# A fixed order for three engines in the second half of an output projection, with three modulation chunks moved behind it and one routing chain in place of two

## Chip, cores and metric

The kernel runs on one core of one Trainium2 chip. The metric is the device time of one execution in microseconds (us). The engines are TensorE (PE; PEld is its weight load), VectorE (DVE), ScalarE (ACT), GpSimd (POOL), and SyncE (SP), whose queue issues the loads of weights. Each engine executes its own list of instructions in order; what an instruction needs from another engine it awaits on a semaphore.

## What is computed

Two layers of a diffusion transformer on 256 latent tokens `x` and 256 context tokens `ctx`, width 1024. Each layer makes six modulation vectors for `x` and six for `ctx` out of the conditioning vectors, mixes tokens (layer 0: a gated linear recurrence beside a spatial gating unit, layer 1: latent attention), adds the result, and then runs a mixture of 32 experts in 4 groups of 8, two experts per token.

```python
for layer in range(DEPTH):
    mx = [m[:, None, :] for m in adaln(c, ada_w[layer], ada_b[layer])]     # 6 vectors
    mc = adaln(c_ctx, ada_w[layer], ada_b[layer])
    ...
    ox, oc = even_mixer(...)            # ends with "@ w_out"
    x = x + mx[2] * ox
    hx2 = modulate(rmsnorm(x, norm_ffn_g[layer]), mx[3], mx[4])
    ctx = ctx + mc[2] * oc
    hc2 = modulate(rmsnorm(ctx, norm_ffn_g[layer]), mc[3], mc[4])
    y = hier_moe(jnp.concatenate([hx2.reshape(-1, d), hc2.reshape(-1, d)], axis=0), *moe_args)
    ...
def hier_moe(...):                       # per token
    p_grp, grp = lax.top_k(softmax(hf @ w_r1 + b_r1), 1)          # 1 group of 4
    p_top, e_top = lax.top_k(softmax(logits2_of_that_group), 2)   # 2 experts of 8
    weight = p_grp * p_top / jnp.sum(p_top)
    ... gather rows by expert, (silu(g) * u) @ w_dn, weighted sum back
```

## The kernel before, in words

Tokens lie in four tiles of 128 (tiles 0 and 1 are `x`, tiles 2 and 3 are `ctx`). The program is written as if in one stream; a scheduler that simulates the engines then decides the order in which each engine's list is laid out, except inside a `manual_schedule` block, where the engines named keep the order in which the code is written.

**The modulations.** 24 chunks of the modulation weights (`ada_w`, 512 columns each, two loads of 1 MB) go through TensorE as many small products (`ada_chunk`, L399: 32 per chunk, then four at L407 for the bias). The accumulators are evacuated to `ada_r` (on ScalarE, or on VectorE with a gain), and GpSimd's queue writes the rows to a DRAM array `mod`. `todo` is the list of chunks, `adaq` those that are loading; `ada_next` runs one and starts the load of another.

**The output projection of layer 0** (L750 to L804) has two halves of 512 output columns. Each operand is split into a high and a low part, so that a product is three (`mm3`, L120 to L122). In the first half the loop runs over the contraction (8 chunks), with all four tiles inside it. In the second half the loop runs over tiles: per tile 8 times 3 products into `acc`, then

- `R.half(t)`: ScalarE squares the first half of the tile's row (L199), VectorE scales the sum (L200);
- `residual(t, 1, acc)`: VectorE multiplies the accumulators by the gate row (L776, `ymix`) and adds the product to the row (L777). A gate row comes by a DMA on ScalarE's queue (L773); there are four such rows for two buffers. In the first half the add is on GpSimd;
- `R.tile(t)`: square of the second half (L206), reciprocal root (L95 to L101), eight transposes (L213), two copies of them by ScalarE (L214, `h2T`), eight products with the router's weights (L217), and the logits (L218, `lg`);
- `R.rows(t, ...)`: the modulated row `h` (L229: VectorE; L230: the add of the shift `rS` on GpSimd), split into a copy by ScalarE and a difference by VectorE (L115 and L116; `hH` and `hL` of the order listings). `rA` and `rS`, the scale and shift rows, are DMAs on ScalarE's queue with one buffer each;
- after tile 3 `R.route`, once for tiles 0 to 2 and once for tile 3: some 30 small steps on VectorE that choose group and experts (`Mb` is the 0/1 table of choices), products that count each token's place in its expert's list (L277, L279, `prk`), the places `cm` (L281), and the weights `wsel`.

The last two chunks of modulations stand behind the loop (L803), and the scheduler may put them earlier.

**The experts** (`moe`). `one_hots(0)` makes the 0/1 matrix `P` from `cm` on VectorE (L856); `gather` (L881) picks rows by products with `P`; then pairs of experts in 16 steps: gate and up (L916), turn (L935), down (L1027), and every second step either a gather or a `combine` (L1046). Expert weights are loaded by SyncE (L849) into 13 buffers of 1 MB. In layer 0 four of these are free only when the projection's pool is closed; the other nine are shared with the chunks of modulations and with the projection's own weights.

Of the kernel before, what the change touches and what calls it, by code (L numbers as in the profile page):

```python
# [16 lines left out]
D = 1024  # L17
# [8 lines left out]
def body(ctx, tc, I, out, dbg=None, stop=None):  # L26
# [60 lines left out]
    def rsqrt(ss, n, inv, base=None):  # L87
# [9 lines left out]
        act(y, y, AF.Exp, scale=-0.5)  # L97
        V.tensor_tensor(a, y, y, op=OP.mult)
# [39 lines left out]
    class Router:  # L138
# [63 lines left out]
        def tile(self, t):  # L202

            cp, Q, c = self.cp, self.Q, t // 2
            ss = sm.tile([128, 1], F32, name="ss", bufs=4)
            act(junk_of(512), xs[t][:, 512:1024], AF.Square, accum_out=ss)  # L206
            rstd = rsqrt(ss, 1, 1.0 / D, self.v0[:, t:t + 1])
# [7 lines left out]
            pl = Q("bt")  # L215
            for k in range(KC):
                mm(pl[:, 0:40], xT[:, k, :], self.wA[c][:, k, :], start=k == 0, stop=k == KC - 1)  # L217
            V.scalar_tensor_tensor(self.lg[:, t, :], pl[:, 0:40], rstd, self.bS[c], op0=OP.mult, op1=OP.add)  # L218
            return rstd

        def rows(self, t, rstd, hs, A=None, S=None):
# [13 lines left out]
        def route(self, t0, t1):  # L235
# [38 lines left out]
            prk = Q("bt", (128, 4, 32))  # L274
            for i in range(NT):
                t = t0 + i
                mm(prk[:, i, :], before, Mb[:, t, :], start=i == 0, stop=t == 0, skip_group_check=True)  # L277
                for u in range(t):
                    mm(prk[:, i, :], ones, Mb[:, u, :], start=False, stop=u == t - 1, skip_group_check=True)  # L279
            cm = self.cm[:, ts]  # L280
            V.scalar_tensor_tensor(cm, prk[:, 0:NT, :], 1.0, Mb[:, ts], op0=OP.add, op1=OP.mult)  # L281

            ge = small([4], "gex")
            V.tensor_tensor(ge, lg[:, :, 0:4], m1[:, :, 0:1].to_broadcast([128, NT, 4]), op=OP.subtract)
            act(ge, ge, AF.Exp)
            gs, gmax = small([1], "gs"), small([1], "gmax")
            V.tensor_reduce(gs[:, :, 0], ge, axis=AX.X, op=OP.add)
            V.tensor_reduce(gmax[:, :, 0], ge, axis=AX.X, op=OP.max)
            V.reciprocal(gs, gs)
            V.tensor_tensor(gs, gs, gmax, op=OP.mult)  # L290
            w1, w2, hw = small([5], "w1"), small([5], "w2"), small([5, 8], "l3")
            V.tensor_tensor(w2, m2, m1, op=OP.subtract)
            act(w2, w2, AF.Exp)
            V.tensor_scalar(w1, w2, 1.0, None, op0=OP.add)
            V.reciprocal(w1, w1)
            V.tensor_tensor(w1, w1, gs.to_broadcast([128, NT, 5]), op=OP.mult)
            V.tensor_tensor(w2, w1, w2, op=OP.mult)
            for h, w in ((hb, w1), (h2, w2)):
                src = h1 if h is hb else h2
                V.tensor_tensor(h.rearrange("p t g e -> p (t g) e"), src.rearrange("p t g e -> p (t g) e"),  # L300
                                w.rearrange("p t g -> p (t g)")[:, :, None].to_broadcast([128, NT * 5, 8]), op=OP.mult)
            V.tensor_tensor(fl(hw), fl(hb), fl(h2), op=OP.add)
            chosen(self.wsel[:, ts], hw)
# [28 lines left out]
    def even_layer(HL, main):  # L332
# [6 lines left out]
        with ExitStack() as st:  # L339
# [53 lines left out]
            def ada_chunk(l, c, w, cols=None):  # L393

                g, half = divmod(c, 2)
                pa = P("ad")
                for k in range(KC):
                    for j in range(4):
                        mm(pa[32 * j:32 * j + 32, 0:128], cst[:, k, :], w[k // 4][:, k % 4, j * 128:(j + 1) * 128],  # L399
                           start=k == 0, stop=cols is not None and k == KC - 1, skip_group_check=True)  # L400
                r = ap.tile([128, 128], F32, name="ada_r", bufs=2)
                if cols is not None:
                    act(r, pa[:, 0:128], AF.Copy)
                    tp(cols[:, c, :], r, ident)
                    return
                for j in range(4):
                    mm(pa[32 * j:32 * j + 2, 0:128], sbi[:, l * 12 + c, :], adab[:, j * 128:(j + 1) * 128],  # L407
                       start=False, stop=True, skip_group_check=True)
                if (l, g) in gains:
# [68 lines left out]
            todo = [(0, c) for c in range(4, 12)] + [(1, c) for c in range(12)]  # L478
# [7 lines left out]
            def ada_next():  # L486
                ada_chunk(*adaq.pop(0))
                ada_ahead()
# [274 lines left out]
        with ExitStack() as st:  # L763
# [714 lines left out]
```

## Time and profile before

| what | value |
|---|---|
| time, median of 3 runs | 1541.81 us (1540.93 to 1544.79) |
| the profiled execution | 1538.64 us, its span 1536.9 us |
| granted TensorE clock, mean | 0.977 of full speed |
| PE busy | 1435.8 us (93% of the span) |
| DVE busy | 662.7 us (43%) |
| ACT busy | 432.5 us (28%) |
| POOL busy | 224.9 us (15%) |
| first product of the second half of layer 0's output projection | 338.7 us |
| first product of the first gather of layer 0's experts | 392.77 us |
| first product with expert weights in layer 0 | 402.36 us |

The span runs from the first to the last instruction; 1.7 us lie around it. The table's last three lines are starts on TensorE, from the span's start. A busy TensorE is not one at its peak: matmuls overlap, and the same matmul takes about twice as long when the granted clock is 0.50.

### The profile page before, as it was taken

To read this page: it belongs to the slowest core of one execution; us is meant where nothing else is said; L and a number is where in the kernel's file an instruction comes from. 1 tells how busy PE (TensorE), PEld (TensorE's weight loads), DVE (VectorE), ACT (ScalarE), POOL (GpSimd) and SP (SyncE) were. 2 spreads that over 40 slices of the span, in tenths; PEclk is the share of its full clock that TensorE was granted. 3 is DMA by queue.
4 is the path that set the end of the run, shared out by engine and by line. 5 is a ranking of instruction groups with operands and counts; after the bars stand their busy time and mean duration, and the time that the engine had idled before them with its cause. 6 is when DMAs were issued, how large, how long until landed. Compare 5 with 4: busy or idle time off the path is not lost. (4 is left out here: it accounts for less than half of the span.)

```text
span 1536.9 us, 21613 instructions
## 1 busy us (share of the span) xinstructions
PE 1435.8 (93%) x8526; PEld 836.2 (54%) x8526; DVE 662.7 (43%) x1494; ACT 432.5 (28%) x984; POOL 224.9 (15%) x250
## 2 busy tenths in 40 slices
PE   6989999999799999999999988997999989999987
PEld 5767777868444554554535356886344434334443
DVE  4455546767424334244423455666232323222222
ACT  4433334543111111211112144453122212212212
POOL 2222222123002012022203221101010100010010
PEclk9999999999899999999999999998999999999999
DMA  9775344785899999999899853135999999999995
GB/s 354 230 248 162 114 144 159 289 298 202 352 406 420 419 421 419 419 420 420 362 417 381 334 226 104 53 99 204 404 420 420 420 419 421 420 421 420 420 420 207
DMA packets 126051, 495.22 MB, mean 322 GB/s; under 512 B 17739, under 2 KB 38636, under 8 KB 77816
## 3 DMA queue, kind: packets, MB, share of 16 engines
q1 hardware_dynamic: 119704, 487.33, 80.3%
q10 hardware_dynamic: 2192, 3.72, 0.7%
q0 software_dynamic: 4048, 2.73, 0.6%
q8 instruction: 70, 1.15, 0.3%
q14 instruction: 37, 0.30, 0.1%
HBM read 492.59 MB, written 1.13 MB: 321 GB/s over the span
## 5 line engine op out<-in xcount | busy, mean ns | idle before, releaser
L916 PE MATMUL gu<-w,xT 128*64 128x512 f32 x2048 | 456.6, 597 | 19.1 <-DMA w<-in_moe_w_gu_dram 13.2
L916 PEld LDWEIGHTS gu<-w,xT 128*64 128x64 f32 x2048 | 151.6, 138 | 313.5 <-issue 273.6
L1027 PE MATMUL dn<-w,hh 128*64 128x512 f32 x960 | 220.2, 606 | 0.0
L924 DVE COPY hh<-gu 128x256 f32<-128x256 f32 x64 | 27.2, 425 | 363.2 <-ACT junk L923 363.2
L1050 POOL TENSOR_TENSOR xx<-xx,z 128x512 f32<-128x512 f32 x56 | 72.8, 1323 | 754.8 <-DVE z L1049 754.8
L1027 PEld LDWEIGHTS dn<-w,hh 128*64 128x64 f32 x960 | 73.7, 139 | 125.1 <-issue 117.9
L923 ACT ACTIVATE junk<-gu 128x256 f32<-128x256 f32 x64 | 24.5, 384 | 397.4 <-PE gu L916 397.4
L120 PE MATMUL mm<-WH,hH 128*128 128x512 f32 x288 | 116.5, 407 | 0.7 <-ACT hH L115 0.7
L121 PE MATMUL mm<-WL,hH 128*128 128x512 f32 x288 | 115.0, 400 | 1.4 <-DVE WL L116 1.4
L122 PE MATMUL mm<-WH,hL 128*128 128x512 f32 x288 | 112.0, 398 | 0.0
L1017 DVE SCALAR_TENSOR_TENSOR y<-dn,ws,y 128x512 fp32r<-128x512 f32 x60 | 45.0, 751 | 145.9 <-ACT y L1016 143.8
L1046 PE MATMUL ad<-y,PT 128*128 128x512 f32 x368 | 95.1, 405 | 5.3 <-DVE z L1049 4.2
L1016 ACT ACTIVATE y<-dn,ws 128x512 fp32r<-128x512 f32 x60 | 41.2, 687 | 176.2 <-PE dn L1027 166.1
L1046 PEld LDWEIGHTS ad<-y,PT 128*128 128x128 f32 x368 | 66.1, 188 | 35.9 <-issue 13.0
L116 DVE TENSOR_TENSOR WL<-w,WH 128x512 fp32r<-128x512 f32 x76 | 56.6, 752 | 54.9 <-ACT WH L115 51.5
L115 ACT ACTIVATE WH<-w 128x512 fp32r<-128x512 f32 x80 | 48.4, 627 | 109.9 <-PE mm L122 86.6
L1049 DVE TENSOR_TENSOR z<-ad,gt 128x512 f32<-128x512 f32 x100 | 66.1, 683 | 14.3 <-PE ad L1046 9.1
L399 PE MATMUL ad<-w,cst 128*32 128x128 f32 x1536 | 60.6, 284 | 6.7 <-DMA w<-in_ada_w_dram 6.7
L120 PEld LDWEIGHTS mm<-WH,hH 128*128 128x128 f32 x288 | 54.8, 190 | 16.9 <-issue 4.0
L121 PEld LDWEIGHTS mm<-WL,hH 128*128 128x128 f32 x288 | 54.8, 190 | 13.0 <-DVE WL L116 1.5
L122 PEld LDWEIGHTS mm<-WH,hL 128*128 128x128 f32 x288 | 54.1, 189 | 12.9 <-issue 1.6
L414 POOL DMA_DIRECT2D mod<-ada_r x80 | 40.4, 512 | 140.1 <-ACT ada_r L412 126.0
(434 smaller groups left out, 1962.3 us busy)
## 6 DMA issues: line engine op xcount, KB each, us to landing
w<-in_moe_w_gu_dram SPq DMA_DIRECT2D x256, 1024.0 KB, 16.3
w<-in_moe_w_dn_dram SPq DMA_DIRECT2D x120, 1024.0 KB, 12.2
w<-in_ada_w_dram SPq DMA_DIRECT2D x48, 1024.0 KB, 7.4
w<-in_ev_w_in_dram SPq DMA_DIRECT2D x32, 256.0 KB, 4.3
w<-in_moe_w_dn_dram SPq DMA_DIRECT2D x16, 512.0 KB, 12.0
w<-in_ev_w_in_dram SPq DMA_DIRECT2D x6, 1024.0 KB, 5.0
w<-in_ev_w_out_dram SPq DMA_DIRECT2D x4, 1024.0 KB, 6.9
w<-in_od_w_out_dram SPq DMA_DIRECT2D x4, 1024.0 KB, 5.1
```

The lines of the kernel that those rows point to most:

```text
L115: act(H, src, AF.Copy)
L116: (eng or V).tensor_tensor(L, src, H, op=OP.subtract)
L120: mm(out, lh, rh, start=start, stop=False, skip_group_check=True)
L121: mm(out, lh, rl, start=False, stop=False, skip_group_check=True)
L122: return mm(out, ll, rh, start=False, stop=stop, skip_group_check=True)
L399: mm(pa[32 * j:32 * j + 32, 0:128], cst[:, k, :], w[k // 4][:, k % 4, j * 128:(j + 1) * 128], start=k == 0, stop=cols is not None and k == ...
L916: mm(gu[64 * c:64 * c + 64, :], xT[:, k, base:base + CAP], w[:, c], start=k == 0, stop=k == KC - 1)
L1017: V.scalar_tensor_tensor(y[:, 1], py, ws, y[:, 0], op0=OP.mult, op1=OP.subtract)
L1027: mm(py[c][64 * par:64 * par + 64, :], hT[par][:, k // 2, k % 2, :], w_[par][:, k % 2, c * 512:(c + 1) * 512], start=k == 0, stop=k == 3)
L1046: mm(cb, PT[:, t, :], y[c][:, i % 2], start=i == 0, stop=i == 2 * len(pend) - 1)
L1049: V.tensor_tensor(z, cb, gate[t // 2][:, hs_], op=OP.mult)
L1050: (V if n % 4 == 3 else nc.gpsimd).tensor_tensor(xs[t][:, hs_], xs[t][:, hs_], z, op=OP.add)
```

## The change

The loop over tiles of the second half becomes one block in which PE, DVE and ACT keep the written order:

- TensorE runs the tiles one after another, `project(t)`, with the transposes (`turn`) and router products (`logits_mm`) of earlier tiles at written places between them.
- The add of the shift `rS` moves from GpSimd to VectorE; `rows` becomes a generator, so that its four steps can be placed one by one. Tile 3's are spread over the tail.
- `rA` and `rS` are issued on GpSimd's queue (`mod_rows`), no longer on ScalarE's.
- One chunk of modulations (`ada_next`) runs before the block, and the last three are kept: the sums of the first in two halves around tile 3's router products, the other two behind it, all ahead of the counting products (`place`). To have three, a third chunk is loaded into buffers of the pool `wxa`, which expert weights used so far. The order of chunks is changed too, so that the last three need no gain and are evacuated by ScalarE.
- `route` is cut into `choose` (with `rest`, the weights) and `place`, and runs once for all four tiles.
- The first `one_hots(0)` of the experts gets high priority. Layer 1's router is written with the new functions; its instructions stand as before.

```diff
@@ even_layer, the second half of the output projection
-            rows, w, WH, WL = {}, ahead[0], [], []
-            for t in range(4):
-                c = t // 2
-                if t % 2 == 0:
-                    rows[c] = (bcast_row(cp, mod[0, 4, c], D, "rA"), bcast_row(cp, mod[0, 3, c], D, "rS"))
-                acc = P("mm")
-                for k in range(KC):
...
-                    mm3(acc, tok(cH, k, t), tok(cL, k, t), WH[k], WL[k], k == 0, k == KC - 1)
-                R.half(t)
-                residual(t, 1, acc)
-                rstd = R.tile(t)
-                if t == 3:
-                    R.route(0, 3)
-                    R.route(3, 4)
-                R.rows(t, rstd, HL.tile(...), *rows[c])
+            mod_rows(0)
+            rstd, rows, xT = {}, {}, {}
+            ada_next()
+            if todo:
+                ada_ahead(wxa[0])
+            assert len(adaq) == 3 and not todo, (len(adaq), len(todo))
+            with tc.manual_schedule(engines={mybir.EngineType.PE, mybir.EngineType.DVE, mybir.EngineType.Activation}):
+                project(0, 0, KC)
+                for t in range(2):
+                    R.half(t)
+                project(1, 0, KC)
+                pl = {}
+                for t in range(4):
+                    residual(t, 1, acc[t])
+                    if t > 1:
+                        R.logits_out(t - 2, rstd[t - 2], pl[t - 2])
+                    ss = R.square(t)
+                    rstd[t] = rsqrt(ss, 1, 1.0 / D, R.v0[:, t:t + 1])
+                    if t == 3:
+                        pl[2] = R.logits_mm(2, xT[2])
+                        xT[3] = R.turn(3)
+                        break
+                    for _ in rows_of(t):
+                        pass
+                    xT[t] = R.turn(t)
+                    if t < 2:
+                        R.half(t + 2)
+                        project(t + 2, 0, KC)
+                        pl[t] = R.logits_mm(t, xT[t])
+                    if t == 1:
+                        mod_rows(1)
+                rows = rows_of(3)
+                next(rows)
+                next(rows)
+                l, c, wc = adaq.pop(0)
+                pa = P("ad")
+                ada_sums(l, c, wc, pa, 0, 4)
+                pl[3] = R.logits_mm(3, xT[3])
+                ada_sums(l, c, wc, pa, 4, KC)
+                for t in (2, 3):
+                    R.logits_out(t, rstd[t], pl[t])
+                next(rows)
+                sums = l, c, pa
+                rest = R.choose(0, 4)
+                while sums:
+                    ada_out(*sums)
+                    sums = ada_chunk(*adaq.pop(0)) if adaq else None
+                next(rows, None)
+                R.place(0, 4)
+            rest()
@@ Router.rows
-            nc.gpsimd.tensor_tensor(h2, h2, S, op=OP.add)
+            yield
+            V.tensor_tensor(h2, h2, S, op=OP.add)
...
-            split(h2, hs[:, 0, :], hs[:, 1, :])
+            yield
+            act(hs[:, 0, :], h2, AF.Copy)
+            yield
+            V.tensor_tensor(hs[:, 1, :], h2, hs[:, 0, :], op=OP.subtract)
```

**Where the rows stand now.** The first place is on ScalarE: the DMA of the fourth gate row, which the residual of tiles 2 and 3 needs (`junk,ss` are squares, `w` is the buffer of the context tiles, `h2T` the copies of transposes). Before:

```order
L773 DMA gate<-mod 128x512
L199 ACTIVATE junk,ss<-xx 128x512
L773 DMA gate<-mod 128x512
L206 ACTIVATE junk,ss<-xx 128x512
L199 ACTIVATE junk,ss<-xx 128x512
L206 ACTIVATE junk,ss<-xx 128x512
L96 ACTIVATE rs_y<-rs_v 128x1
L199 ACTIVATE junk,ss<-w 128x512
L97 ACTIVATE rs_y<-rs_y 128x1
L96 ACTIVATE rs_y<-rs_v 128x1
L97 ACTIVATE rs_y<-rs_y 128x1
L214 ACTIVATE h2T<-bt 128x512 x2
```

And of the change:

```order
L96 ACTIVATE rs_y<-rs_v 128x1
L97 ACTIVATE rs_y<-rs_y 128x1
L256 ACTIVATE hL_3683<-h_3684 128x1024
L226 ACTIVATE h2T<-bt 128x512 x2
L201 ACTIVATE junk,ss<-w 128x512
L818 DMA gate<-mod 128x512
L214 ACTIVATE junk,ss<-w 128x512
L96 ACTIVATE rs_y<-rs_v 128x1
L97 ACTIVATE rs_y<-rs_y 128x1
L256 ACTIVATE hH_3763<-h_3764 128x1024
```

The fourth gate's DMA stood before all second-half squares and ahead of the copies; now it stands behind tile 1's `hL` copy and transposes.

The second place is on VectorE: from tile 0's residual on. Before:

```order
L776 TENSOR_TENSOR ymix<-mm,gate 128x512 x2
L777 TENSOR_TENSOR xx<-xx,ymix 128x512
L776 TENSOR_TENSOR ymix<-mm,gate 128x512
L777 TENSOR_TENSOR xx<-xx,ymix 128x512
L95 SCALAR_TENSOR_TENSOR rs_v<-ss,v_767 128x1
L200 TENSOR_SCALAR v_767<-ss 128x1
L95 SCALAR_TENSOR_TENSOR rs_v<-ss,v_767 128x1
L200 TENSOR_SCALAR v_767<-ss 128x1
L98 TENSOR_TENSOR rs_a<-rs_y 128x1
L99 TENSOR_TENSOR rs_a<-rs_a,rs_v 128x1
L98 TENSOR_TENSOR rs_a<-rs_y 128x1
L100 TENSOR_SCALAR rs_a<-rs_a 128x1
```

And of the change:

```order
L821 TENSOR_TENSOR ymix<-mm,gate 128x512
L822 TENSOR_TENSOR xx<-xx,ymix 128x512
L95 SCALAR_TENSOR_TENSOR rs_v<-ss,v_767 128x1
L100 TENSOR_TENSOR rs_a<-rs_y 128x1
L101 TENSOR_TENSOR rs_a<-rs_a,rs_v 128x1
L102 TENSOR_SCALAR rs_a<-rs_a 128x1
L103 TENSOR_TENSOR rs_y<-rs_y,rs_a 128x1
L250 SCALAR_TENSOR_TENSOR h_3611<-xx,rs_y,rA 128x1024
L252 TENSOR_TENSOR h_3611<-h_3611,rS 128x1024
L258 TENSOR_TENSOR hH_3610<-h_3611,hH_3610 128x1024
L202 TENSOR_SCALAR v_767<-ss 128x1
L821 TENSOR_TENSOR ymix<-mm,gate 128x512
```

The reciprocal roots of tiles 0 and 1 were woven into each other; now tile 0 is carried to the end, shift add and split included, before tile 1's residual begins.

The third place is on TensorE: from the last product of the projection to the counting products. Before:

```order
L213 MATMUL bt<-ident,w 128x128 x8
L399 MATMUL ad<-w,cst 32x128 x17
L407 MATMUL ad<-adab,sbi 2x128 x4
L217 MATMUL bt<-wA_3416,h2T 128x40 x4
L213 MATMUL bt<-ident,w 128x128 x2
L217 MATMUL bt<-wA_3416,h2T 128x40 x4
L213 MATMUL bt<-ident,w 128x128 x6
L399 MATMUL ad<-w,cst 32x128 x16
L217 MATMUL bt<-wA_3416,h2T 128x40 x8
L399 MATMUL ad<-w,cst 32x128 x16
L407 MATMUL ad<-adab,sbi 2x128 x4
```

And of the change:

```order
L235 MATMUL bt<-wA_3407,h2T 128x40 x8
L225 MATMUL bt<-ident,w 128x128 x8
L235 MATMUL bt<-wA_3416,h2T 128x40 x8
L225 MATMUL bt<-ident,w 128x128 x8
L441 MATMUL ad<-w,cst 32x128 x16
L235 MATMUL bt<-wA_3416,h2T 128x40 x8
L441 MATMUL ad<-w,cst 32x128 x16
L447 MATMUL ad<-adab,sbi 2x128 x4
L441 MATMUL ad<-w,cst 32x128 x32
L447 MATMUL ad<-adab,sbi 2x128 x4
L441 MATMUL ad<-w,cst 32x128 x32
L447 MATMUL ad<-adab,sbi 2x128 x4
```

Behind tile 3's router products stood 16 products of a chunk and its bias; now there stand 16, 32 and 32 products of three chunks, each with its bias.

## Rows read from the trace of the kernel before

**Rows 1.** Stretches: us, busy us by engine, granted PE clock, DMA share, GB/s.

```profile
342.00:369.30 27.30, 27.30 (x132) 22.34 (x132) 19.96 (x37) 7.98 (x22) 9.35 (x8) 0.94 0.59 232
...
379.40:386.80 7.40, 7.40 (x87) 6.03 (x77) 6.42 (x33) 1.58 (x4) 2.40 (x2) 0.50 0.59 220
...
392.77:396.30 3.53, 3.53 (x16) 3.53 (x17) 1.28 (x2) 0.00 (x0) 0.20 (x1) 0.50 0.92 358
396.50:402.36 5.86, 5.86 (x53) 5.79 (x52) 1.38 (x2) 0.60 (x1) 0.14 (x1) 1.00 1.00 420
402.36:756.00 353.64, 349.50 (x1798) 170.40 (x1795) 126.97 (x214) 68.81 (x157) 40.93 (x30) 1.00 1.00 415
```

**Rows 2.** TensorE's waits, 402 to 756 us: total us, times, longest.

```profile
PE bt L935 <- DVE hh L927: 2.1, 1, 2.1
...
PEld gu L916 <- DMA w<-in_moe_w_dn_dram: 1.1, 4, 0.3
```

**Rows 3.** TensorE in order of time: start, us (a product of f32 operands counts twice).

```profile
365.22 1.87 PE L217 MATMUL bt<-wA,h2T 128*128 128x40 f32 x16
...
373.01 1.28 PE L399 MATMUL ad<-w,cst 128*32 128x128 f32 x34
...
380.77 3.64 PE L217 MATMUL bt<-wA,h2T 128*128 128x40 f32 x16
384.34 1.94 PE L399 MATMUL ad<-w,cst 128*32 128x128 f32 x32
386.21 0.60 PE L407 MATMUL ad<-adab,sbi 24*2 24x128 f32 x8
...
390.94 0.21 PE L277 MATMUL bt<-Mb,before 128*128 128x32 bf16 x1 [3.38 <-DVE Mb L269]
...
392.77 0.80 PE L881 MATMUL ad<-P,hH 128*128 128x256 f32 x2 [1.54 <-DVE P L856]
...
402.36 13.95 PE L916 MATMUL gu<-w,xT 128*64 128x512 f32 x64
```

**Rows 4.** VectorE in order of time: start, us, instruction, idle before.

```profile
347.43 0.68 DVE L776 TENSOR_TENSOR ymix<-mm,gate 128x512 f32<-128x512 f32 x1
352.66 0.69 DVE L776 TENSOR_TENSOR ymix<-mm,gate 128x512 f32<-128x512 f32 x1 [4.55 <-issue]
...
360.33 3.46 DVE L229 SCALAR_TENSOR_TENSOR h<-xx,rs_y,rA 128x1024 f32<-128x1024 f32 x1
...
372.28 0.68 DVE L777 TENSOR_TENSOR w<-w,ymix 128x512 f32<-128x512 f32 x1
...
373.75 1.45 DVE L95 SCALAR_TENSOR_TENSOR rs_v<-ss,v 128x1 f32<-128x1 f32 x1 [0.62 <-ACT junk L206]
...
376.82 1.28 DVE L229 SCALAR_TENSOR_TENSOR h<-w,rs_y,rA 128x1024 f32<-128x1024 f32 x1
378.02 1.22 DVE L116 TENSOR_TENSOR hH<-h,hH 128x1024 fp32r<-128x1024 f32 x1
...
379.44 0.28 DVE L259 TENSOR_REDUCE m<-lg 128x15 f32<-128x120 f32 x1
...
384.45 0.26 DVE L218 SCALAR_TENSOR_TENSOR lg<-bt,rs_y,bS 128x40 f32<-128x40 f32 x1 [0.83 <-PE bt L217]
...
391.50 1.22 DVE L856 TENSOR_TENSOR P<-iota,cm 128x1024 fp32r<-128x1024 f32 x1
```

**Rows 5.** ScalarE in order of time: start, us, instruction.

```profile
373.00 0.63 ACT L206 ACTIVATE junk<-w 128x512 bf16<-128x512 f32 x1 [2.71 <-DVE w L777]
...
375.91 1.04 ACT L115 ACTIVATE hH<-h 128x1024 fp32r<-128x1024 f32 x1
...
377.38 1.08 ACT L214 ACTIVATE h2T<-bt 128x512 f32<-128x512 f32 x2 [0.25 <-PE bt L213]
```

**Rows 6.** GpSimd in order of time: the shift add of one tile.

```profile
360.31 2.40 POOL L230 TENSOR_TENSOR h<-h,rS 128x1024 f32<-128x1024 f32 x1 [10.24 <-DVE rs_y L101]
```

**Rows 7.** The tile `gate`: from a DMA's issue to its landing.

```profile
DMA to landing us min/median/max: 3.7/5.2/6.7
```

More of the change, by code (lines that the diff above doesn't have):

```diff
@@ L97, in rsqrt @@
         act(y, y, AF.Exp, scale=-0.5)
+        if mid is not None:
+            mid()
         V.tensor_tensor(a, y, y, op=OP.mult)
@@ L229, in rows, with place, choose @@
             V.scalar_tensor_tensor(h2, xs[t], rstd, A, op0=OP.mult, op1=OP.mult)
-            nc.gpsimd.tensor_tensor(h2, h2, S, op=OP.add)
+            yield
+            V.tensor_tensor(h2, h2, S, op=OP.add)
             if t == 0:
                 dump(f"h2_{self.l}", h2)
-            split(h2, hs[:, 0, :], hs[:, 1, :])
-        def route(self, t0, t1):
+            yield
+            act(hs[:, 0, :], h2, AF.Copy)
+            yield
+            V.tensor_tensor(hs[:, 1, :], h2, hs[:, 0, :], op=OP.subtract)
+        def place(self, t0, t1):
+            Mb = self.Mb
+            prk = self.Q("bt", (128, 4, 32))
+            for t in range(t0, t1):
+                i = t - t0
+                mm(prk[:, i, :], before, Mb[:, t, :], start=i == 0, stop=t == 0, skip_group_check=True)
+                for u in range(t):
+                    mm(prk[:, i, :], ones, Mb[:, u, :], start=False, stop=u == t - 1, skip_group_check=True)
+            V.scalar_tensor_tensor(self.cm[:, t0:t1], prk[:, 0:t1 - t0, :], 1.0, Mb[:, t0:t1], op0=OP.add, op1=OP.mult)
+        def choose(self, t0, t1):
             NT, cp, Q, lg, l = t1 - t0, self.cp, self.Q, self.lg[:, t0:t1], self.l
@@ L272, in route @@
             chosen(Mb[:, ts], hb)
[L274 to L301, printed above, removed]
@@ L305, in blocks @@
+            return rest
         def blocks(self, cp, Q):
@@ L399, in ada_chunk, with ada_sums @@
                         mm(pa[32 * j:32 * j + 32, 0:128], cst[:, k, :], w[k // 4][:, k % 4, j * 128:(j + 1) * 128],
-                           start=k == 0, stop=cols is not None and k == KC - 1, skip_group_check=True)
+                           start=k == 0, stop=k == KC - 1, skip_group_check=True)
                 r = ap.tile([128, 128], F32, name="ada_r", bufs=2)
-                if cols is not None:
-                    act(r, pa[:, 0:128], AF.Copy)
-                    tp(cols[:, c, :], r, ident)
+                act(r, pa[:, 0:128], AF.Copy)
+                tp(cols[:, c, :], r, ident)
+            def ada_sums(l, c, w, pa, k0=0, k1=KC):
+                for k in range(k0, k1):
+                    for j in range(4):
+                        mm(pa[32 * j:32 * j + 32, 0:128], cst[:, k, :], w[k // 4][:, k % 4, j * 128:(j + 1) * 128],
+                           start=k == 0, stop=False, skip_group_check=True)
+                if k1 < KC:
                     return
+                g, half = divmod(c, 2)
                 for j in range(4):
@@ L408, in ada_chunk, with ada_out @@
                        start=False, stop=True, skip_group_check=True)
+                return l, c, pa
+            def ada_out(l, c, pa):
+                g, half = divmod(c, 2)
+                r = ap.tile([128, 128], F32, name="ada_r", bufs=2)
                 if (l, g) in gains:
@@ L476, in load_head @@
                 return r
-            todo = [(0, c) for c in range(4, 12)] + [(1, c) for c in range(12)]
+            todo = [(0, c) for c in range(4, 12)] + [(1, c) for c in (8, 9, 0, 1, 2, 3, 4, 5, 6, 7, 10, 11)]
             adaq = []
@@ L783, in even_layer, with mod_rows, project @@
                 residual(t, 0, acc0[t])
[L784 to L790 removed]
+            w, WH, WL, acc = ahead[0], [], [], {}
+            rA, rS = {}, {}
+            def mod_rows(c):
+                rA[c], rS[c] = (bcast_row(cp, mod[0, i, c], D, n, eng=nc.gpsimd) for i, n in ((4, "rA"), (3, "rS")))
+            def project(t, k0, k1):
+                if k0 == 0:
+                    acc[t] = P("mm")
+                for k in range(k0, k1):
                     if t == 0:
@@ new lines, in rows_of @@
+            def rows_of(t):
+                return R.rows(t, rstd[t], HL.tile([128, 2, D], F32R, name=("hH0", "hL0", "hH1", "hL1")[t]), rA[t // 2], rS[t // 2])
+            mod_rows(0)
[47 more added lines that the diff above has]
+                R.place(0, 4)
@@ L1419, in odd_layer @@
                     rstds.append(R.tile(t))
-                R.route(0, 2)
+                rest = R.choose(0, 2)
+                R.place(0, 2)
+                rest()
                 for t in range(2):
-                    R.rows(t, rstds[t], HL.tile([128, 2, D], F32R, name=f"s{t}"))
+                    for _ in R.rows(t, rstds[t], HL.tile([128, 2, D], F32R, name=f"s{t}")):
+                        pass
         return R
```

55 lines of the change are left out of this document (45 added, 10 removed).

## Prediction

> **What bounds the kernel now.** I read the stretches first, to see which engine is full where. From 402.36 us on, the first twelve steps of layer 0's experts keep TensorE busy for 349.5 of 353.6 us [rows 1], and TensorE's waits say that nearly none of the rest is for weights: the longest wait is 2.1 us for VectorE, those for loads sum to 1.1 us [rows 2]. DMA is full there too (share 1.00, 415 GB/s), but it is ahead. So whatever moves the first expert product at 402.36 moves everything behind it by as much; a stretch ahead of it is worth its full length.
>
> Next, how that product comes about. TensorE is full through the second half of the projection, 27.3 of 27.3 us [rows 1], that is 6.8 us per tile. After it the line of work leaves TensorE: tile 3's row is complete at 372.96 (the add at 372.28) [rows 4], its router products run 380.77 to 384.41 at the lower clock [rows 3], its logits stand at 384.45, `P` at 391.50 [rows 4], the gather begins at 392.77 and lasts 9.6 us [rows 3]. The granted clock in these stretches is what the reader should note: 0.50 (1.2 GHz) from 379.4 to 396.3, and 1.00 (2.4 GHz) after [rows 1].
>
> **The change, part by part.** I carry the line of work from tile 0 to the gather, with durations of the rows.
>
> *Tile 0 starts sooner.* TensorE no longer runs tiles 0 and 1 in turns. VectorE was idle for 4.55 us before tile 0's residual at 352.66, and its last work ahead of it ends at 348.1 [rows 4]. TensorE's list now gives it tile 0's 24 products alone, so the residual can start at 348.1. I allow 0.6 us for GpSimd's adds of the first half: a VectorE operation with two operands in SBUF took 3.46 us instead of 1.28 beside GpSimd's add at 360.31 [rows 4, 6]. Tile 0's row is complete at 348.1 + 0.6 + 2 x 0.7 = 350.1 instead of 354.1: a gain of 4.0 us.
>
> *Each tile is now one closed chain on VectorE.* From a complete row to the next one, in written order: square on ScalarE and the way to `rs_v` 0.8 (372.96 to 373.75); `rs_v` itself 0.15 (1.45 less the 1.3 for which GpSimd held it); root and its four corrections 1.62 (375.20 to 376.82); `h` 1.28; the shift add, now on VectorE, 1.22 by the row of its size; ScalarE's copy 1.04; the difference 1.22; the next tile's multiply and add 1.4 [rows 4, 5]. Sum 8.7 us. In the schedule before, pieces of other tiles filled these gaps; now VectorE idles through them. The shift add itself is a gain: GpSimd took 2.40 for it and could hold VectorE by up to 2.2 [rows 4, 6].
>
> Two of the three passages cost more. VectorE scales the first-half square of the tile after next before it goes on, and ScalarE makes that square behind the two copies of transposes: 1.08 + 0.8 against the 1.22 of VectorE's difference, 0.7 late [rows 4, 5]. Tile 1 is complete at 350.1 + 9.4 = 359.5, tile 2's chain is due at 368.9.
>
> *The fourth gate row comes late.* Its DMA is now behind tile 1's copies on ScalarE (order, first place), so it is issued just when VectorE wants the row. Landing takes 3.7 to 6.7 us [rows 7]; queued behind VectorE's wait are tile 2's residual and all that follows. I take 4.4, toward the low end, because the projection's weights are all in by then and the queue is quiet. Tile 2 is complete at 373.3, tile 3 with its 8.7 and one logits step of 0.26 at 382.3, against 372.96 before: 9.3 us later.
>
> *Router products and the kept chunks.* Behind tile 3's row: square, root, two copies of transposes, 0.8 + 0.15 + at most 1.3 of the 1.62 + 1.08 = 3.4 us, then the router products. TensorE by then has had some 10 us with little to do, since its last projection product comes by 348.1 + 3 x 6.8 = 368.5; in the trace its clock fell at 379.4 though it had been busy for most of the ten microseconds before. So 3.64 us, as in the row, and not 1.87 [rows 3]. Tile 3's logits stand at 382.3 + 3.4 + 3.6 + 0.3 = 389.6.
>
> Then TensorE has, ahead of the counting products, 16 + 32 + 32 products with three biases (order, third place). A trace row counts each twice, so a chunk is two rows of 32. At the lower clock 5 x 1.94 + 3 x 0.60 = 11.5, and 0.6 for two handovers of the one accumulator: 401.4. At the upper clock 160 x 0.038 + 3 x 0.4 + 0.6 = 7.9: 397.2 [rows 3].
>
> VectorE meanwhile has the chain of choices for four tiles: twelve steps in series of 0.28 to 0.35, ten small ones between at half of that, four masks: about 5.5; then tile 3's difference 1.22 and the weights 1.2, which stand ahead of `cm`: 397.5 [rows 4]. One chain in place of two saves VectorE some 3 us of steps, but nothing now waits for it longer than for TensorE.
>
> From the counting products to the gather it is 392.77 - 390.94 = 1.8 us before [rows 3]; with twice the products 2.3. Lower clock: 401.4 + 2.3 = 403.7, which is **10.9 us** later. Upper clock: VectorE decides, 397.5 + 0.3 + 1.3 = 399.1, **6.3 us** later.
>
> I take the lower clock. The row that is nearest is 379.40 to 386.80: TensorE was busy for all 7.40 us with just these chunk and router products, and the clock stayed 0.50; it rose only during the gather [rows 1]. The Trainium skill, "TensorE: Matmul & The Clock Gate", Part 1, says the opposite for dense work: the throttled state is the default and activity releases it. By that rule three chunks in a row bring the clock up and 6.3 is the result; the trace does not bear it out for this mixture, but no row has two whole chunks without router products between them.
>
> *At nothing:* `rA` and `rS` on GpSimd's queue (wanted 8 us after issue; if late, the landing of a gate row's size again, 4 us); layer 1's router (rows unchanged); the high priority (`P` stood first before). The third chunk takes two load buffers early, and six are kept until its sums: 6 MB, 15 us at 415 GB/s [rows 1]. The last two come free at about 401 and are wanted by the second expert 7 us after the first product at 413, so they are hidden; uncovered they would cost 5.
>
> **Sum.** The profiled execution took 1538.64 us. With 10.9 it would be 1549.5. The median of the three runs, 1541.81, lies 3.2 above that execution, and 10.9 on top of it is 1552.7. I say 1551.
>
> **Rivals.** *The kept chunks raise the clock* (above): 6.3, that is 1546.5 between the same two bases. For it: fully dense products; against it: the 7.40 us at 0.50.
>
> *Faster.* The fixed order lets VectorE keep TensorE's pace of 6.8 us a tile, the gate lands in time, and the clock stays up. Then tile 3 is complete at 350.1 + 20.4 = 370.5, logits 3.4 + 1.9 + 0.3 later at 376.1, TensorE's chunks end at 384.0, VectorE at 384.0, gather at 386: 7 us sooner, 1533. It decides at a pace of about 9 us a tile with the clock up and no gate wait; every price of the two pushes it over. Against it is the written order itself: no work of another tile stands in the 0.8, the 1.0 and the root's gaps.
>
> *No change to measure.* The gate row lands in time and the clock comes up, at 8.7 to 9.4 a tile: the gather then starts within 2 us of 392.77. Or the delay is taken up later; but TensorE never waits for weights in the experts, so it can't be made good there [rows 2].
>
> **Chances.** Lower clock 0.55; clock raised, VectorE bounds 0.25; no change 0.11; faster 0.09. This kernel's runs tell about 0.3% (4.6 us) from no change. The first two are slower: 0.80. For the range I leave out the faster case and the half of no change below zero: from 1541, up to 1557, which holds the lower clock with a gate of 6.7 (2.3 more) and 2 us of handovers.
>
> **What would show it.** Right: VectorE idle before tile 2's `ymix` until a gate lands, some 4 us; starts of `h` 9 us apart or more; the clock at 0.50 from before tile 3's transposes; counting products right behind the last bias, after 400; the gather near 403. Wrong: `h` starts 7 us apart, the chunks at 1.0 us per 32 rows, or TensorE waiting for loads after the first expert.

## The result and the profile after

The changed kernel takes 1552.54 us (median of 4 runs, 1551.06 to 1554.3) against 1542.14 for the kernel before in the same session (4 runs, 1540.93 to 1544.79). The ratio is 1.0066, with a 95% interval from 1.0047 to 1.0084: slower by 10 us. The profiled execution of the changed kernel took 1554.3 us, with a span of 1552.5.

VectorE of the changed kernel in order of time, as [rows 4]:

```profile
353.64 1.28 DVE L250 SCALAR_TENSOR_TENSOR h<-xx,rs_y,rA 128x1024 f32<-128x1024 f32 x1
...
357.37 1.23 DVE L258 TENSOR_TENSOR hH<-h,hH 128x1024 fp32r<-128x1024 f32 x1 [1.19 <-ACT hH L256]
...
362.73 1.29 DVE L250 SCALAR_TENSOR_TENSOR h<-xx,rs_y,rA 128x1024 f32<-128x1024 f32 x1
...
371.36 0.69 DVE L821 TENSOR_TENSOR ymix<-mm,gate 128x512 f32<-128x512 f32 x1 [3.23 <-DMA gate<-mod]
372.09 0.69 DVE L822 TENSOR_TENSOR w<-w,ymix 128x512 f32<-128x512 f32 x1
...
375.06 1.28 DVE L250 SCALAR_TENSOR_TENSOR h<-w,rs_y,rA 128x1024 f32<-128x1024 f32 x1
...
380.64 0.69 DVE L822 TENSOR_TENSOR w<-w,ymix 128x512 f32<-128x512 f32 x1
...
390.14 0.26 DVE L240 SCALAR_TENSOR_TENSOR lg<-bt,rs_y,bS 128x40 f32<-128x40 f32 x1 [3.87 <-PE bt L235]
...
397.35 0.50 DVE L305 TENSOR_TENSOR wsel<-l,h 128x32 f32<-128x32 f32 x4
402.04 0.29 DVE L269 SCALAR_TENSOR_TENSOR cm<-bt,Mb 128x128 f32<-128x128 f32 x1 [4.20 <-PE bt L268]
```

`h` starts 9.1 us apart for tiles 0 and 1; in front of tile 2 VectorE stands still for 3.23 us until the gate row lands; tile 3's row is complete at 381.33, 8.4 us behind [rows 4]. At the end VectorE has done its choices and weights at 397.85 and waits 4.20 us for the counting products. What TensorE did meanwhile, as [rows 3]:

```profile
379.29 3.63 PE L235 MATMUL bt<-wA,h2T 128*128 128x40 f32 x16 [5.24 <-ACT h2T L226]
382.72 1.95 PE L225 MATMUL bt<-ident,w 128*128 128x128 f32 x8
384.60 1.94 PE L441 MATMUL ad<-w,cst 128*32 128x128 f32 x32
386.47 3.64 PE L235 MATMUL bt<-wA,h2T 128*128 128x40 f32 x16
...
397.46 3.64 PE L441 MATMUL ad<-w,cst 128*32 128x128 f32 x64 [0.40 <-ACT ada_r L457]
401.03 0.60 PE L447 MATMUL ad<-adab,sbi 24*2 24x128 f32 x8
401.56 0.24 PE L266 MATMUL bt<-Mb,before 128*128 128x32 bf16 x2
...
403.74 0.49 PE L977 MATMUL ad<-P,hH 128*128 128x256 f32 x2 [1.73 <-DVE P L952]
```

After a gap of 5.24 us it runs router products, transposes and the three kept chunks back to back, all at lower-clock lengths. The stretches, as [rows 1]:

```profile
379.29:401.72 22.43, 21.64 (x261) 17.63 (x262) 13.12 (x47) 4.80 (x12) 4.01 (x8) 0.50 0.50 177
...
413.20:767.00 353.80, 349.49 (x1803) 170.98 (x1801) 128.38 (x216) 69.08 (x157) 40.90 (x30) 1.00 1.01 420
```

The gather starts at 403.74, 10.97 us later than [rows 3], the first expert product at 413.20, 10.84 later. The first step of the experts takes 25.48 us instead of 26.85, since no stretch at the lower clock lies in it (before, the clock was at 0.50 from 420.3 to 423.8). The next ten steps run as they did, and at their end the difference is 9.6 us. It changes once more at the branch behind the twelve steps. The first products behind it, of the changed kernel and then of the kernel before:

```profile
778.46 16.73 PE L1012 MATMUL gu<-w,xT 128*64 128x512 f32 x64 [4.99 <-PEq L1274]
```

```profile
767.13 13.95 PE L916 MATMUL gu<-w,xT 128*64 128x512 f32 x64 [3.22 <-PEq L1177]
```

The wait is 1.8 us longer, and the products behind it run partly at the lower clock. From there to the end the two executions stay 15 to 16 us apart. Why one execution of each differs by more than the medians do is asked by a control below (c0).

The queue of weight loads had a wait of its own ahead of the experts; the longest in 330 to 402 us (total, times, longest), of the changed kernel and of the kernel before:

```profile
SPq L945 <- PE ad L441: 48.2, 5, 39.0
```

```profile
SPq L325 <- PE ad L399: 29.1, 2, 25.1
SPq L849 <- PE ad L399: 8.3, 4, 4.2
```

The experts' loads (L945) stood 39 us in one piece behind the kept chunks' products, whose buffers they need. From 280 us to the first expert product the DMA moved 133.2 us x 247 GB/s = 32.9 MB, against 122.4 x 287 = 35.1 MB before.

### The profile page after: what moved, and what is told of

Its sections match the earlier page's. It is cut to its first block, busy times and chain, and to the rows that moved or that the text cites. A ratio compares the mean times of both kernels' runs of the same rounds, so it can differ in the third digit from the quotient of the medians.

```text
span 1552.5 us, 21588 instructions
## 1 busy us (share of the span) xinstructions
PE 1446.9 (93%) x8526; PEld 842.8 (54%) x8526; DVE 659.8 (42%) x1472; ACT 433.0 (28%) x982; POOL 217.4 (14%) x250
## 5 line engine op out<-in xcount | busy, mean ns | idle before, releaser
L1145 DVE TENSOR_TENSOR z<-ad,gt 128x512 f32<-128x512 f32 x100 | 66.0, 682 | 13.5 <-PE ad L1142 10.2
L441 PE MATMUL ad<-w,cst 128*32 128x128 f32 x1280 | 54.1, 298 | 4.9 <-DMA w<-in_ada_w_dram 3.7
## 6 DMA issues: line engine op xcount, KB each, us to landing
w<-in_moe_w_dn_dram SPq DMA_DIRECT2D x16, 512.0 KB, 13.9
```

The lines of the kernel that those rows point to most:

```text
L1145: V.tensor_tensor(z, cb, gate[t // 2][:, hs_], op=OP.mult)
```

## The experiments

All twelve, by the start of the experts' first gather (the expectations call it the last gather), TensorE's wait at the branch, and the time (medians; the ratio is to the kernel before in the same session, with its 95% interval). The first two columns are of one profiled execution each. e1 to e4 ran in one session, c0 and e5 to e7 in a second, e8 to e11 in a third, so times of different sessions are best compared by their ratios:

| kernel | gather, us | branch wait, us | time, us | ratio |
|---|---|---|---|---|
| before | 392.77 | 3.22 | 1542.14 | |
| changed | 403.74 | 4.99 | 1552.54 | 1.0066 (1.0047 to 1.0084) |
| e1 gate row early | 393.53 | 5.84 | 1545.28 | 1.0030 (1.0016 to 1.0044) |
| e2 products in the gap | 394.79 | 5.72 | 1545.51 | 1.0035 (1.0021 to 1.0049) |
| e3 two chunks in the gap | 395.65 | 3.18 | 1547.50 | 1.0040 (1.0025 to 1.0055) |
| e4 gate early, woven | 386.64 | 5.62 | 1538.25 | 0.9987 (0.9975 to 0.9999) |
| c0 before again | 393.12 | 3.12 | 1545.15, one run | |
| e5 = e4, one chunk ahead | 386.46 | 3.10 | 1533.26 | 0.9971 (0.9948 to 0.9993) |
| e6 = e4, two chunks ahead | 391.07 | 3.24 | 1537.65 | 0.9982 (0.9967 to 0.9997) |
| e7 no fixed order | 389.88 | 3.08 | 1536.45 | 0.9964 (0.9951 to 0.9978) |
| e8 = e5, squares early | 387.04 | 3.37 | 1535.11 | 0.9963 (0.9945 to 0.9981) |
| e9 changed, one chunk ahead | 399.26 | 3.08 | 1549.28 | 1.0060 (1.0040 to 1.0080) |
| e10 = e7, gate early, one ahead | 387.54 | 3.13 | 1534.79 | 0.9956 (0.9937 to 0.9975) |
| e11 = e7, add on GpSimd | 394.81 | 3.10 | 1545.31 | 1.0034 (1.0018 to 1.0049) |

**e1, the gate row early.**

```diff
-                    gates[half] = cp.tile([128, 512], F32, name="gate", bufs=2)
+                gates[half, c] = cp.tile([128, 512], F32, name="gate", bufs=3)
...
+            for c in range(2):
+                gate_row(c, 1)
             w, WH, WL, acc = ahead[0], [], [], {}
```

> Both gate rows of the second half are fetched ahead of the fixed block (a third buffer), nothing else is changed. Theory (a closed chain on VectorE carries the late row to the end): VectorE's 3.23 us wait before tile 2's residual goes, tile 2 and tile 3 come 3.2 sooner, and as the products behind tile 3 keep their clock and length, the last gather starts at 400.5 instead of 403.74 and the time is 3.2 us below the changed kernel's. Rival (TensorE's tail or ScalarE's order sets the end by itself): another wait takes the place of this one, the gather stays within 1 us of 403.7 and the time within 1 us.

The wait is gone, and tile 3's row is complete at 376.56, 4.8 us sooner (1.5 of these because tile 0 was sooner in this execution). But the gather came 10.2 sooner, not 3.2. Its TensorE rows show why:

```profile
374.51 3.63 PE L235 MATMUL bt<-wA,h2T 128*128 128x40 f32 x16 [3.68 <-ACT h2T L226]
...
381.69 2.33 PE L235 MATMUL bt<-wA,h2T 128*128 128x40 f32 x16
383.95 1.08 PE L441 MATMUL ad<-w,cst 128*32 128x128 f32 x32
```

and its stretches:

```profile
374.51:382.00 7.49, 7.49 (x58) 6.68 (x58) 5.66 (x12) 3.40 (x8) 0.00 (x0) 0.50 0.01 2
384.00:392.00 8.00, 6.26 (x195) 4.75 (x194) 7.68 (x36) 0.99 (x4) 4.01 (x8) 1.00 0.87 335
```

The gap ahead of tile 2's router products is 3.68 instead of 5.24 us, and the clock is back at 2.4 GHz by 384, ahead of most of the chunks; in the changed kernel it came back at 401.7. The late row cost its 3.2 us directly, and in these executions it went with some 5 more from the clock. Both theories had missed that.

**e2, products in the gap.**

```diff
                     xT[t] = R.turn(t)
+                    if t == 2:
+                        pa = P("ad")
+                        for _ in range(4):
+                            ada_sums(*adaq[0], pa, 0, 4)
```

> The first half of the first kept chunk (16 products) is computed four extra times in TensorE's 5.24 us gap behind tile 2's transposes; the real sums overwrite them, so the result is the same and TensorE only has more to do. Theory (TensorE's lower clock is part of the delay, and it fell because TensorE had nothing to do there): the granted clock stays 1.00 up to the chunks behind tile 3, router products take 1.87 instead of 3.64 and 32 products 1.9 instead of 3.64, VectorE then bounds, and the gather starts at 396 to 398, 6 to 7.5 us sooner. Rival (the clock falls whatever stands in the gap, or this kind of product doesn't hold it): rows of 3.64 as in the changed kernel, the extra products take up to 7.8 us at the lower clock and push tile 2's router products back, gather at 403.7 to 406.5.

```profile
373.21 5.16 PE L441 MATMUL ad<-w,cst 128*32 128x128 f32 x128
378.37 1.98 PE L235 MATMUL bt<-wA,h2T 128*128 128x40 f32 x16
...
382.63 1.98 PE L235 MATMUL bt<-wA,h2T 128*128 128x40 f32 x16
...
394.79 0.40 PE L980 MATMUL ad<-P,hH 128*128 128x256 f32 x2 [2.63 <-DVE P L955]
```

More work on TensorE, and the gather 8.95 us sooner, more than the 6 to 7.5 expected. The clock fell all the same, at 372.8, just ahead of the added products, but it was back at 376.3, within them, and stayed at 1.00 up to the gather; in the changed kernel it was at 0.50 from 374.5 to 401.8. Tile 2's row was complete 0.9 sooner here; the other 8 us go with the clock, since all the rest of the work is the same.

**e3, two chunks in the gap.**

```diff
                         pl[t] = R.logits_mm(t, xT[t])
+                    if t == 2:
+                        ada_out(*ada_chunk(*adaq.pop(0)))
+                        ada_out(*ada_chunk(*adaq.pop(0)))
```

> Two of the three kept chunks are moved from behind tile 3's router products into TensorE's gap behind tile 2's transposes; one stays behind. Theory (the three chunks ahead of the counting products are the largest part of the delay, since VectorE has finished its choices at 397.9 and waits 4.2 us for the counts): TensorE's tail gets 8 to 9 us shorter, VectorE bounds, and the gather starts at 395 to 398. Rival A (the chunks run at the lower clock in the gap as well, 4.2 us each): tile 2's router products and tile 3's transposes are 3 to 4 us late, gather at 399 to 401. Rival B (the tail isn't what VectorE's counts wait for in the end, the choices are): gather within 1 us of 403.7.

The gather is in the theory's range at 395.65: the counting products now wait 3.66 us for VectorE's `Mb`, so TensorE's tail no longer bounds. A new wait took part of the gain: ScalarE's copy of a chunk's sums stands behind its copy of tile 2's high part in the written order, so the second chunk waited 3.47 us for the accumulator, and tile 3's root 3.17 for ScalarE.

**e4, gate early and woven.** `mid` runs a tile's difference between the root's two parts of the next tile:

```diff
-                    rstd[t] = rsqrt(ss, 1, 1.0 / D, R.v0[:, t:t + 1])
+                    rstd[t] = rsqrt(ss, 1, 1.0 / D, R.v0[:, t:t + 1], mid=lambda: next(rows, None))
...
-                    for _ in rows_of(t):
-                        pass
                     xT[t] = R.turn(t)
+                    rows = rows_of(t)
+                    next(rows)
+                    next(rows)
```

> As the first of these, and VectorE's list is woven: a tile's low part (difference) stands in the gap of the next tile's root, and ScalarE copies a tile's transposes before the high part. Theory (the closed chain of 8.7 to 9.4 us per tile is what makes tile 3 late): h starts come 6.8 to 7.2 us apart, tile 3's row is complete at 372 to 375 instead of 381.33, and with the chunks still behind it the gather starts at 395 to 398. Rival (the gate row alone explains tile 3's lateness, weaving gives nothing beyond it): gather at 400.5 as with the gate alone. Rival B (TensorE, 6.8 us a tile with router products and transposes between, sets the pace): h 8 us apart, gather at 398 to 400.

```profile
351.53 1.28 DVE L250 SCALAR_TENSOR_TENSOR h<-xx,rs_y,rA 128x1024 f32<-128x1024 f32 x1
...
359.76 1.28 DVE L250 SCALAR_TENSOR_TENSOR h<-xx,rs_y,rA 128x1024 f32<-128x1024 f32 x1
...
367.94 1.28 DVE L250 SCALAR_TENSOR_TENSOR h<-w,rs_y,rA 128x1024 f32<-128x1024 f32 x1
...
374.70 1.28 DVE L250 SCALAR_TENSOR_TENSOR h<-w,rs_y,rA 128x1024 f32<-128x1024 f32 x1
```

8.2, 8.2 and 6.8 us apart instead of 9.1, 9.0 and 8.5 in e1; only the last passage is as short as the theory had it, the first two are as rival B had them. Tile 3's row is complete at 371.8, TensorE had no gap to speak of and kept its clock, and all three chunks were done at 383.5, before VectorE wanted the counts. The gather starts 6.1 us before that of the kernel before and 8 us before the theory's range, which had left the clock low. But the time gains only 2 us: the branch wait is 5.62.

**c0, the kernel before once more.**

> The kernel before, unchanged, profiled once more: how far one execution stands for the others at the branch behind layer 0's twelve steps. There its first profile has 3.22 us of waiting on TensorE and 13.95 us for the first 64 products behind it; the changed kernel's has 4.99 and 16.73, and the three other variants profiled so far with all three chunks kept to the end have 5.6 to 5.8 and 16.5 to 16.7. Theory (the branch is late there because the weights' transfers are late): 3.2 to 3.5 us again. Rival (chance from execution to execution): 5 us or more, and 16.5, here too.

The wait is 3.12 as before, but the 64 products behind it took 15.65 us and not 13.95: by the next step this execution is 2.8 us behind the first, and at its end 6.5. So in these two executions the length of the wait repeats and the clock behind it does not. The profiled execution of before was a quick one (its median is 3.2 us above it), and the 15.66 us between the two profiled executions are no measure of the change.

**e5 and e6, chunks ahead of the block** (e6 takes two):

```diff
-            assert len(adaq) == 3 and not todo, (len(adaq), len(todo))
+            ada_out(*ada_chunk(*adaq.pop(0)))
+            assert len(adaq) == 2 and not todo
```

> As the woven kernel with the early gate, and one of the three kept chunks is computed ahead of the fixed block, so two stay behind. Theory (a kept chunk holds two load buffers; the queue of weight loads waited 29.5 us in one piece for its products, and the experts' transfers, which run at the full 420 GB/s, never make that up): the loads go on earlier, 2 MB more have landed by 400 us, TensorE's wait at the branch behind the twelve steps falls from 5.62 to 3.2 to 3.5 us, and although TensorE gets 3 us more work ahead of the block, the time is 3 to 5 us below the woven kernel's, 1533 to 1535. Rival (only the start of the first expert product counts, the branch costs what it costs): the gather starts 0 to 3 us later than 386.64 and the time is 0 to 3 us above the woven kernel's.

> The same with two of the three chunks ahead of the block. TensorE has 6 us more ahead of the fourth tile's products, which VectorE can't hide: the gather at 389 to 390. Theory (the transfers decide): 4 MB more have landed by 400 us than in the woven kernel, and in spite of the later gather the time is within 2 us of the kernel with one chunk ahead. Rival (the gather decides): 3 us slower than the woven kernel.

The first product behind the branch, in e4 and in e5:

```profile
763.19 16.74 PE L1020 MATMUL gu<-w,xT 128*64 128x512 f32 x64 [5.62 <-PEq L1282]
```

```profile
760.80 13.95 PE L1021 MATMUL gu<-w,xT 128*64 128x512 f32 x64 [3.10 <-PEq L1283]
```

Both start their experts within 0.2 us of each other. By then e4 has moved 31.0 MB since 280 us and e5 33.4; e4 reaches the branch with its transfers late, e5 doesn't, and its median is 5.0 us lower. The wait at the branch is what the rival (the branch costs what it costs) had wrong. The gain in time is likely but not separated: the intervals of the two ratios overlap. e6 has 35.8 MB and the same short wait, and is 4.4 us slower than e5 by medians for a gather that is 4.6 later (its profiled execution was the longest of its twelve, and these intervals overlap too). So once the transfers are in time the gather seems to decide, and my theory that earlier loads would still pay was wrong there. Its rival was wrong as well: against the woven kernel e6 is not 3 us slower but level, with a later gather and a shorter wait.

**e7, no fixed order.**

```diff
-            with tc.manual_schedule(engines={mybir.EngineType.PE, mybir.EngineType.DVE, mybir.EngineType.Activation}):
+            if True:
```

> The changed kernel with the fixed order of the three engines taken away; the scheduler orders the same operations, with the kept chunks, the single chain of choices and the adds on VectorE left as they are. Theory (the written order, with its closed chain per tile and its late gate row, makes tile 3 late): tile 3's row is complete at 371 to 375 instead of 381.33, and the gather starts at 392 to 397; time 1540 to 1546. Rival (the kept chunks and the single chain make the delay, whatever the order): gather at 400 or later, time 1549 or more.

Beyond what I expected: the gather is 13.9 us sooner than in the changed kernel, 2.9 sooner than before, and the time 16.1 us below the changed kernel's and below before's. Tile 3's row is complete at 373.0, and the scheduler has laid the chunks between transposes and router products:

```profile
362.00:385.00 23.00, 22.54 (x276) 18.91 (x275) 18.73 (x41) 8.56 (x20) 5.13 (x10) 1.00 0.45 153
```

TensorE is full and at 1.00 in the stretch in which it starves in the changed kernel.

**e8, squares early.**

```diff
                 project(1, 0, KC)
+                for t in range(2, 4):
+                    R.half(t)
...
-                    if t < 2:
-                        R.half(t + 2)
```

> As the woven kernel with the early gate and one chunk ahead; in addition ScalarE makes the first-half squares of tiles 2 and 3 ahead of the tiles' chains instead of behind the copies of transposes, where VectorE waited 1.5 us for them on two passages. Theory: h starts 7 us apart instead of 8.2, tile 3's row complete at 368.5 to 370 instead of 371.9, gather 2 to 3 us before 386.46, time 1530 to 1532. Rival (TensorE's projection products or the experts' transfers bound by now): gather within 1 us of 386.46, time within 1 us of the kernel without this edit.

`h` starts 6.6, 6.6 and 7.0 us apart, as the theory has it, but the first one starts 2.3 us later than in e5, and tile 3's row is complete at 372.3. The gather agrees with the rival (0.6 later). The medians are 1.9 us apart, more than its 1 us, but the intervals of the ratios overlap nearly whole: no gain to measure.

**e9, the changed kernel with one chunk ahead** (the edit of e5 alone).

> The changed kernel as it is (closed chain, late gate row), with one of its three kept chunks computed ahead of the fixed block. Theory of the held buffers: TensorE's wait at the branch behind the twelve steps falls from 4.99 to 3.1 to 3.3 us; theory of TensorE's tail: it ends 4.6 us sooner, and VectorE, done at 397.9, then bounds, so the gather starts at 399 to 400 (or at 393 to 395, if the clock also comes back): time 1543 to 1548. Rival (both cost nothing): gather at 403 or later, wait 5 us, time 1551 or more.

The branch wait falls to 3.08, the gather to 399.26, with VectorE done at 398.0 as bound: both theories hold in the profile. The clause in brackets does not: the clock came back, at 388.6, within tile 3's router products, but tile 3's row was 1.4 us later in this execution (the third gate row held VectorE for 3.06 us), so its logits stood at 390.5, as in the changed kernel. The time, 1549.28, is 1.3 above the range, and its interval overlaps the changed kernel's; the gain stays within what these runs can tell. The ten executions lie from 1543.49 to 1556.10, the shortest at the highest mean clock (0.976) and the longest at the lowest (0.965), so one profile doesn't tell the clock of the others.

**e10, no fixed order, gate early, one chunk ahead** (the edits of e7, e1 and e5).

> The changed kernel without the fixed order, with the gate rows early and one chunk ahead: the scheduler's own order with the same two mends that the woven kernel has. Theory (the scheduler's order is limited by TensorE's 6.8 us a tile, not by a chain): gather at 387 to 389, 1 to 3 us sooner than without the mends (389.88), time 1533 to 1536. Rival (a written woven order is needed for more): no change from 389.88 and 1536.5.

Gather at 387.54 and 1534.79 us, as the theory has it. It beats the kernel before; from e5, e7 and e8 its interval doesn't separate it.

**e11, the shift add back on GpSimd, no fixed order.**

```diff
-            V.tensor_tensor(h2, h2, S, op=OP.add)
+            nc.gpsimd.tensor_tensor(h2, h2, S, op=OP.add)
```

> The changed kernel without the fixed order, with the shift add back on GpSimd. Theory (GpSimd's add takes 2.40 instead of 1.22 us and holds VectorE by up to 2.2): gather 1 to 4 us behind 389.88, time 1537.5 to 1540.5. Rival (VectorE is relieved of four adds of 1.22, and nothing waits for GpSimd's): gather 0 to 3 us sooner, time 1534 to 1536.5.

4.9 us of gather and 8.9 of time against e7, more than the theory asked. One of GpSimd's adds, the VectorE operation that ran beside it, and one that ran beside the next such add (368.15 to 370.50):

```profile
359.01 2.37 POOL L252 TENSOR_TENSOR h<-h,rS 128x1024 f32<-128x1024 f32 x1 [1.99 <-DVE h L250]
```

```profile
359.45 3.01 DVE L258 TENSOR_TENSOR hH<-h,hH 128x1024 fp32r<-128x1024 f32 x1
...
368.64 2.41 DVE L822 TENSOR_TENSOR w<-w,ymix 128x512 f32<-128x512 f32 x1
```

3.01 instead of 1.22 and 2.41 instead of 0.69. TensorE's clock was at 0.50 from 374.3 to 398.2, so part of the 4.9 is the clock again.

## Why the prediction was right, step by step

The forecast was 1551, in a range of 1541 to 1557, slower with 0.80. The measured 1552.54 came about by the case held likeliest. That the sum fits so closely is in part luck, twice over: tile 0 came 1.25 us late and the gate cost 1.2 less than I had it, and of the gather's 10.97 us the experts' first step gave back 1.4 and the branch added 1.8.

- *TensorE full in the experts, so the start of the first product is passed on.* Right: behind the first step the difference is 9.5 to 9.6 us up to the branch, and the medians moved by 10.4.
- *Tile 0 complete at 350.1.* 351.35 in the changed kernel; 349.2 to 350.1 in e1 to e4. I had VectorE as the bound; in the changed kernel it waited 1.49 us for tile 0's last product. The granted clock had been at 0.50 up to 347.2 there, and in e1, whose tile 0 was complete at 349.9, up to 344.9.
- *Chain of 8.7 us, 9.4 on two passages.* Rows complete 9.1 (tile 0 to 1) and 8.55 us (2 to 3) apart. Right. e4 and e8 confirm that the order makes the gaps: woven, the same operations follow at 6.6 to 8.2.
- *Gate row 4.4 us late.* 3.23: issued at 365.37, in use 6.0 later; VectorE came 0.6 later and the row 0.5 sooner than I had them. In e1 no other wait took its place.
- *Lower clock through the kept chunks.* Right: counting products at 401.56 (said 401.4), gather 403.74 (said 403.7). The Trainium skill, "TensorE: Matmul & The Clock Gate", Part 1, has activity releasing the throttle; the changed kernel speaks against it, with TensorE busy for 21.64 of 22.43 us at 0.50, and e1 and e2 for it, where the clock came back under such products.
- *The price of that clock, 10.9 against 6.3, is the term that I mis-sized.* I gave the clock 4.6 us; e2 measured some 8. At the lower clock tile 2's router products (3.63 instead of 1.98) stand ahead of tile 3's transposes, which began 1.4 us after their row was complete; transposes and the 16 products behind them are slower too. Tile 3's logits stood at 390.4, in e2 at 385.5. I had left VectorE's end at 397.5 in both cases; in e2 choices and weights are done at 393.0.
- *Held load buffers at nothing.* Wrong in part. The loads waited 39 us for the chunks, 2.2 MB less had landed, and the 420 GB/s of the experts didn't make that up by the branch: the wait there is 1.8 us longer, and in e4 it is 2.5 longer than in e5. My 5 us for the uncovered case was too much.
- *Shift add on VectorE a gain.* Right, and larger than I made it (e11).
- *One chain of choices.* Neutral to slightly dear: logits to `P` 7.05 us before [rows 4], 7.94 in e1, where VectorE bounds and tile 3's difference stands in it.
- *The rival "faster"* was set against the fixed order, and that is where it failed. Without that order (e7) the rest of the change is faster than before, by 0.36%.

So the fixed order costs 13.9 us of the gather's start by e7, more than the whole loss, and the change's other parts give 2.9 back. How much of the 13.9 is chain, gate row and clock can't be added up, since in e1 and e2 a shorter or filled gap came with an earlier return of the clock.

Why the branch waits longer where transfers are late can be read off the DMA records. These are the last microsecond of TensorE's work ahead of the branch, in the kernel before and in the changed one (the last two numbers are the DMA's share and GB/s):

```profile
762.91:763.91 1.00, 1.00 (x4) 0.47 (x3) 0.95 (x2) 0.00 (x0) 1.00 (x1) 1.00 0.33 139
```

```profile
772.47:773.47 1.00, 1.00 (x4) 0.47 (x3) 0.94 (x2) 0.00 (x0) 1.00 (x1) 1.00 1.04 434
```

Behind TensorE's last product comes one packet of 16 KB of the kind `instruction`: 0.37 us behind it in the kernel before, 2.22 us in the changed one, and in both the first product behind the branch starts 2.8 us after this packet. All fourteen profiles agree. In the ten with short waits the transfers had sunk to 139 to 279 GB/s in that microsecond, and the packet starts 0.37 to 0.39 us behind the last product; in the four with long waits (changed, e1, e2, e4) they still ran at 418 to 434, and it starts 2.2 to 3.0 us behind. The product follows 2.7 to 3.0 us after the packet in all. So the longer wait goes with a later load of code, in each case while weights were still being moved; what holds the packet back is not shown.

What stays open: e3 and e11 took 3.7 and 2.7 us more than their gathers explain, with short waits; the intervals of their times reach some 2.3 us to either side, which is less than that.

## What to carry to other kernels

A written order for several engines should have the next tile's work in each gap of a tile's chain: without it the scheduler's order was better here by 13.9 us of the gather's start, with it (e5) the two were level. Read the chain from row to row and compare it with the feeding engine's pace. Where TensorE starves, price the starving twice, once as the wait and once as the clock at which everything behind it runs, and give the second as a range. And work kept back to fill a wait keeps its load buffers too, so ask which loads stand behind it, and whether a branch comes before they have caught up.

## What the runs showed that was not expected

- The clock did not go by the length of TensorE's wait alone. In the changed kernel it fell at 374.5, 0.5 us into the 5.24 us wait, and stayed at 1.2 GHz to 401.8, through 22 us of nearly unbroken work. In e1 (3.68 us of waiting) the same kinds of products were back at 2.4 GHz at 382.5. In e9, which waited longer (4.17 us ahead of tile 2's transposes and 4.42 behind them), they were back at 388.6. With the gap filled (e2) the clock fell while TensorE worked and was back 3.5 us later. What decides between these is not shown.
- The same kernel loses 2.8 us or none at the branch from one execution to the next by the clock alone (13.95 or 15.65 us for 64 products, behind waits of 3.2 and 3.1). Behind the branch the clock was at 0.50 from 785.6 to 789.0 in the first execution, and from 768.3 to 771.7 and 785.3 to 792.2 in the second.
